# Seven block products instead of eight in the up product of a ConvGeGLU feed-forward stage

## The chip, the cores and the metric

One core of one Trainium2 chip. The metric is device time in microseconds (us) of one execution of the whole kernel; the kernel before takes 887.17 us (median of 3 runs, 887.15 to 887.45).

## The reference

One layer of a hybrid encoder on 512 tokens of width 1024, in float32: a Mamba-2 mixer and an RG-LRU mixer side by side, merged by gates and projected (`w_out`), with a residual; then a feed-forward block. The change lies in the feed-forward block, the last part:

```python
h = rmsnorm(x, ffn_pre_norm[l])                       # [512 tokens, 1024]
up = causal_dwconv(h @ w_ffn_up[l], ffn_conv_w[l], ffn_conv_b[l])   # 6144 channels, 3 taps
f_gate, f_val = jnp.split(up, 2, axis=-1)             # 3072 each
f = (gelu(f_gate, approximate=True) * f_val) @ w_ffn_down[l]
x = x + rmsnorm(f, ffn_post_norm[l])
```

## The kernel before

All large products run in `float32r`. To keep float32 accuracy each operand is split in two, `hi` (a rounded copy, written by ScalarE) and `lo` (what is left, source minus `hi`, by VectorE), and a product is three matmuls: hi x hi, hi x lo, lo x hi (`mm3`, L85). Every matmul has a weight load of its own.

The weights are one stream of slabs of 128x1024 numbers, 512 KB each (`slabs`). `load_slab` (L146) issues the transfer on the SP queue, up to three slabs ahead; `split_slab` (L153) has ScalarE write `whi`, and the low part is queued in `late` and subtracted by VectorE in `low_parts` (L178, L180). `slab` (L182) hands out the next slab and splits ahead. VectorE, ScalarE and TensorE keep the order in which the program is written (`InOrder`, L40; the helper's line is L50), so an instruction that waits holds everything behind it on its engine. GpSimd builds a few constants at the start.

The up stage computes 48 column tiles of 128 channels in pairs: tile i of the gate half and tile i of the value half, 24 pairs (L852). The activations h2 are kept channel-major and split, `h2T` (L797), [128 channels, 8 contraction tiles, 512 tokens]. `up_product` (L828) is one slab against all 512 tokens: 8 contraction tiles x 3 terms = 24 matmuls of 512 columns into one PSUM bank. The first four up products are cut in two halves of 256 tokens: the first halves run as soon as the first two token tiles are normed (L819 to L825, EARLY = 4), the second halves in `up_product`. Behind each product `conv` (L218) has ScalarE scale and shift the PSUM tile into a `tmp` tile and VectorE add the other two taps, reading PSUM. ScalarE then does the gelu of the gate (L855), VectorE multiplies it with the value (L856), and `split` (L195, L197) writes the result as two tiles, which the down product reads as its stationary operand (`facts`, L840).

The down stage is `norm_add` (L700) with 12 slabs per half of the output columns. `use_sqrt` (L864) has ScalarE ready for square roots before it. The slabs are [2 contraction tiles, 512 columns]; each is multiplied for four token tiles. The last three slabs of the second half are taken token tile by token tile, with the norm and the store behind each.

Of the kernel before, what the change touches and what calls it, by code (L numbers as in the profile page):

```python
# [8 lines left out]
F32 = mybir.dt.float32  # L9
F32R = mybir.dt.float32r  # L10
# [24 lines left out]
# columns of the row parameter array  # L35
# [4 lines left out]
class InOrder:  # L40
    """An engine whose instructions keep the order in which they are written here."""
# [12 lines left out]
def block_kernel(ctx: ExitStack, tc, x, slabs, wgate, pc, rows, out):  # L54
    nc = tc.nc
    V, A, PE = (InOrder(tc, e) for e in (nc.vector, nc.scalar, nc.tensor))
    G = nc.gpsimd

# [54 lines left out]
    def step(cost, fn, *args):  # L113
        """A step for the vector engine, of that many microseconds."""
        steps.append((cost, fn, args))

    def next_slab():
        """What follows needs the tensor engine to have gone on, or another engine's result."""
        steps.append(None)
# [21 lines left out]
    n_slabs = slabs.shape[0]  # L141
    stream = {"load": 0, "split": 0, "use": 0}
    raws, splits, places, late = {}, {}, {}, []
    AHEAD, EARLY, WARM = 2, 4, 24

    def load_slab():  # L146
        i = stream["load"]
        if i < n_slabs:
            raws[i] = wts.tile([P, D], F32, tag="raw", name="raw")
            nc.sync.dma_start(out=raws[i], in_=slabs[i])  # L150
            stream["load"] += 1

    def split_slab():  # L153
        i = stream["split"]
        if i >= n_slabs:
            return
        while stream["load"] <= i:
            load_slab()
        raw = raws.pop(i)
        if i == DT_SLAB:  # L160
            hi, lo = wts.tile([P, D], F32R, tag="whi", name="whi"), None
            A.copy(hi, raw)
            h3, r3 = (a.rearrange("p (k c) -> p k c", k=KT)[:, :, 16:32] for a in (hi, raw))
            V.tensor_sub(h3, r3, h3.bitcast(F32))
        else:
            if i in places:
                hi, lo = places[i]()
            else:
                hi = wts.tile([P, D], F32R, tag="whi", name="whi")
                lo = wts.tile([P, D], F32R, tag="wlo", name="wlo")  # L170
            A.copy(hi, raw)
            late.append((lo, raw, hi.bitcast(F32)))
        splits[i] = hi, lo
        stream["split"] += 1
        while stream["load"] < min(n_slabs, stream["split"] + 3):
            load_slab()
# [14 lines left out]
    def prefetch(n):  # L191
        while stream["split"] < min(n_slabs, stream["use"] + n):
            split_slab()
# [54 lines left out]
    def inv_rms(parts, width, e):  # L248
        """(sum of parts / width + e) ** -0.5, as two factors; one part may be [128, n]."""
# [48 lines left out]
    def causal(value, name):  # L298
        m = const.tile([P, P], F32, name=name)      # value where column >= row
# [193 lines left out]
    def carry(c, g):  # L493
        """What earlier chunks bring to this one, and the state after it."""
# [205 lines left out]
    def norm_add(acts, n_slab, e, row, res, tail, lead, target, done):  # L700
        """target = res + RMSNorm(acts @ W) * row; token tile by token tile over the last slabs."""
# [136 lines left out]
    f16 = {}  # L838

    def facts(k):  # L840
        if k < 8:
            kind, key, w = "H", 0, 8
        elif k < 16:
            kind, key, w = "L", 1 + (k - 8) // 4, 4
        else:
            kind, key, w = "Y", 3, 8
        if key not in f16:
            f16[key] = tuple(big16(kind, F32R) if w == 8 else lru8(F32R) for _ in range(2))
        hi, lo = f16[key]
        return hi[:, k % w, :], lo[:, k % w, :]  # L850

    for i in range(NF):  # L852
        gt = conv(up_product(), C_FCW + 3 * i, C_FCB + i, 3)
        vt = conv(up_product(), C_FCW + 3 * (NF + i), C_FCB + NF + i, 3)
        A.activation(gt, gt, AF.Gelu_apprx_tanh)  # L855
        V.tensor_mul(gt, gt, vt)  # L856
        split(*facts(i), gt)

    row_post2 = row_tile(R_POST2)
# [5 lines left out]
    norm_add(facts, 12, EPS1, row_post2, x1s, 3, 0, lambda c, h: tmp(), store)  # L865
# [5 lines left out]
def _layout(x, mix_pre_norm, mix_post_norm, w_in, ssm_conv_w, ssm_conv_b, ssm_dt_bias, ssm_a_log,  # L871
# [5 lines left out]
    def cols(w):  # L877
        """[1024, 128 n]: slab j holds [row in tile, row tile, column] of its 128 columns."""
# [3 lines left out]
    def rws(w):  # L882
        """[K, 1024]: per column half, slabs of two 128-row tiles by 512 columns."""
# [10 lines left out]
    dts = np.zeros((1, P, KT, 8, HEADS), np.float32)     # the dt columns twice, then zeros  # L894
# [17 lines left out]
    def chan(v, n):  # L912
        """[taps, 128 n] to [128, n, taps]."""
# [28 lines left out]
```

## Time and profile before

| | |
|---|---|
| median of 3 runs | 887.17 us |
| span of the profiled execution | 885.8 us |
| median less that span | 1.37 us |
| TensorE busy | 872.5 us, 98% |
| VectorE busy | 519.9 us, 59% |
| ScalarE busy | 392.8 us, 44% |
| GpSimd busy | 1.7 us |
| granted TensorE clock, mean | 0.999 |

The profile is of one execution. It lists its span, from its first to its last instruction; the time of a run also covers what lies around that. PE is TensorE's matmuls, PEld its weight loads, DVE VectorE, ACT ScalarE, POOL GpSimd, SPq the queue of SP, from which the transfers are issued. In a timeline the ends of matmuls are modelled and neighbours overlap, so spacing is read from starts. "L50" is the helper that keeps program order, and stands for the line of most VectorE, ScalarE and TensorE instructions.

### The profile page before, as it was taken

What the parts mean: (1) busy time and instruction counts of PE and PEld (TensorE: products, weight loads), DVE (VectorE), ACT (ScalarE), POOL (GpSimd) and SP (SyncE); (2) the same over time, 40 slices, a digit from 0 to 9 for tenths busy, and PEclk for the clock granted to TensorE, in tenths of its full rate; (3) what the DMA queues carried; (4) which work ended last, traced back from release to release, by engine and by line L of the source; (5) the groups of instructions that cost most, each with busy time, mean ns of one, the idle gap of its engine ahead of it and who ended that gap; (6) DMA issues with size and microseconds to landing.
All of it is one profiled execution on the core that took longest, in us unless ns stands there. A gap on an engine that the chain in (4) does not pass through costs nothing.

```text
span 885.8 us, 10176 instructions
## 1 busy us (share of the span) xinstructions
PE 872.5 (98%) x4050; PEld 724.0 (82%) x4050; DVE 519.9 (59%) x732; ACT 392.8 (44%) x602; POOL 1.7 (0%) x14
## 2 busy tenths in 40 slices
PE   7999999999999999999999999999999999999996
PEld 6888887888878888888888988888888888888885
DVE  6777657987874554344467566666666666223225
ACT  6454535579584334222355444444444444213222
POOL 0000000000000000000000000000000000000000
PEclk9999999999999999999999999999999999999999
DMA  6332232222325332222370022222222222322212
GB/s 224 102 137 95 95 118 84 92 87 72 142 96 182 128 119 72 96 95 95 102 252 27 25 94 96 95 95 96 95 95 95 95 95 95 117 98 95 95 48 96
DMA packets 26192, 91.61 MB, mean 103 GB/s; under 512 B 3040, under 2 KB 4256, under 8 KB 25632
## 3 DMA queue, kind: packets, MB, share of 16 engines
q1 hardware_dynamic: 26144, 90.95, 30.1%
q8 instruction: 32, 0.52, 0.2%
q14 instruction: 16, 0.13, 0.0%
HBM read 88.81 MB, written 2.13 MB: 103 GB/s over the span
## 4 chain that ended last, share of the span: by engine, by line
PE 88%; DVE 5%; ACT 5%; issue 1%; DMA 1%; SPq 0%; DVEq 0%; ACTq 0%
PE ps L50 88%; ACT L L50 1%; DVE L L642 1%; DMA raw<-slabs 1%; DVE wlo L180 1%; ACT whi L50 1%; ACT tmp L50 1%; DVE tmp L660 0%; DVE L L636 0%; ACT L50 0%; ACT junk L245 0%; ACT M L50 0%; DVE Y L197 0%; ACT Y L50 0%; ACT junk L50 0%
## 5 line engine op out<-in xcount | busy, mean ns | idle before, releaser
L180 DVE TENSOR_TENSOR wlo<-raw,whi 128x1024 fp32r<-128x1024 f32 x139 | 169.7, 1222 | 140.5 <-ACT whi L50 137.9
L50 PE MATMUL ps<-C,whi 128*128 128x512 f32 x768 | 241.6, 389 | 0.0
L50 PE MATMUL ps<-H,whi 128*128 128x512 f32 x720 | 224.1, 394 | 1.5 <-DVE H L50 1.5
L50 ACT CAST whi<-raw 128x1024 fp32r<-128x1024 f32 x137 | 143.0, 1045 | 110.9 <-PE ps L50 105.6
L50 PEld LDWEIGHTS ps<-C,whi 128*128 128x128 f32 x768 | 144.1, 188 | 29.9
L225 DVE SCALAR_TENSOR_TENSOR tmp<-ps,pcs,tmp 128x511 f32<-128x511 f32 (+1 forms) x156 | 116.6, 748 | 80.4 <-ACT tmp L50 77.9
L50 PE MATMUL ps<-C,wlo 128*128 128x512 f32 x416 | 161.8, 389 | 0.0
L50 PEld LDWEIGHTS ps<-H,whi 128*128 128x128 f32 x720 | 134.1, 188 | 31.1 <-issue 2.4
L50 PE MATMUL ps<-H,wlo 128*128 128x512 f32 x352 | 137.5, 391 | 0.4 <-DVE wlo L180 0.3
L50 ACT ACTIVATE tmp<-ps,pcs 128x512 f32<-128x512 f32 x68 | 53.1, 780 | 128.2 <-PE ps L50 128.2
L50 PEld LDWEIGHTS ps<-C,wlo 128*128 128x128 f32 x416 | 78.1, 188 | 16.1
L50 PE MATMUL ps<-whi,H 128*128 128x512 f32 x256 | 81.4, 394 | 0.0
L50 PEld LDWEIGHTS ps<-H,wlo 128*128 128x128 f32 x352 | 66.1, 188 | 15.2 <-DVE wlo L180 1.2
L50 PE MATMUL ps<-whi,Y 128*128 128x512 f32 x192 | 59.6, 389 | 0.0
L50 PEld LDWEIGHTS ps<-whi,H 128*128 128x128 f32 x256 | 48.1, 188 | 10.3 <-issue 0.5
L50 PE MATMUL ps<-wlo,H 128*128 128x512 f32 x128 | 49.9, 389 | 0.0
L50 ACT CAST Y<-tmp 128x512 fp32r<-128x512 f32 x24 | 14.9, 621 | 66.9 <-DVE tmp L690 36.8
L50 ACT ACTIVATE tmp<-ps,halfb 128x512 f32<-128x512 f32 x32 | 21.5, 687 | 49.6 <-PE ps L50 49.6
L50 PEld LDWEIGHTS ps<-whi,Y 128*128 128x128 f32 x192 | 36.0, 188 | 7.5
L50 PE MATMUL ps<-Y,whi 128*128 128x512 f32 x128 | 40.5, 396 | 0.2 <-DVE Y L197 0.2
L50 PE MATMUL ps<-whi,L 128*128 128x512 f32 x128 | 39.7, 389 | 0.0
L50 PE MATMUL ps<-wlo,Y 128*128 128x512 f32 x96 | 37.3, 389 | 0.0
(167 smaller groups left out, 848.1 us busy)
## 6 DMA issues: line engine op xcount, KB each, us to landing
raw<-slabs SPq DMA_DIRECT2D x149, 512.0 KB, 3.2
quad<-x SPq DMA_DIRECT2D x8, 512.0 KB, 4.3
M<-acsD SPq DMA_DIRECT2D x4, 1024.0 KB, 4.6
out<-tmp SPq DMA_DIRECT2D x8, 256.0 KB, 2.1
wg<-wgate SPq DMA_DIRECT2D x8, 128.0 KB, 3.3
quad<-rows SPq DMA_DIRECT2D x2, 512.0 KB, 4.7
pcs<-pc SPq DMA_DIRECT2D x1, 178.0 KB, 7.1
acsD<-acsT SPq DMA_DIRECT2D x1, 32.0 KB, 2.9
```

The lines of the kernel that those rows point to most:

```text
L50: return lambda *args, **kw: self.tc.keep_in_program_order(op(*args, **kw))
L180: V.tensor_sub(*late.pop(0))
L225: V.scalar_tensor_tensor(out=t[:, d:], in0=acc[:, :S - d], scalar=pcs[:, w:w + 1], in1=t[:, d:], op0=ALU.mult, op1=ALU.add)
L642: V.tensor_tensor_scan(out=qq[:, e, :], data0=aa[:, e, :], data1=uu[:, e, :], initial=0.0, op0=ALU.mult, op1=ALU.add)
```

## The change

Two slabs of a pair are read as a matrix of 2 x 2 blocks: slab pair (gate, value) by depth half (contraction tiles 0 to 3 and 4 to 7), a11, a12, a21, a22. The activations are cut in depth half by token half. For pairs 3 to 23 the up product of a pair is formed from seven products of blocks ([128 channels x 512 deep] by [512 deep x 256 tokens]) in Winograd's form of Strassen's scheme. Pairs 0 to 2 stay as they were (`PLAIN = 3`).

For the weights it forms s1 = a21 + a22, s2 = s1 - a11, s4 = a11 - a21, s3 = a12 - s2 per pair, on GpSimd, which gets a program-ordered handle `GP`. Seven blocks are split (s1, s2, s3, s4, a11, a12, a22): `hi` on ScalarE, `lo` on VectorE for five and on GpSimd for a12 and a22. For the activations it once rebuilds h2 from its two parts (`h_whole`, eight adds of 128x512 on GpSimd), forms four combinations (`h_sums`, four of 128x1024) and splits them (`h_split`).

The products of a pair are added up by VectorE and ScalarE into two SBUF tiles, `oa` (gate) and `ob` (value), which `conv` now reads in place of PSUM. `seven` spreads a pair over seven slots, one block product each; the splits for the next pair, and the conv, gelu and multiplication of the pair before, are written between them. A pair's last block product (a22) runs in slot 4 of the next pair. The weights of a pair come by one transfer of 1 MB into one half of a two-pair ring.

The results of the up stage are kept unsplit (`f_tile`), and `f_split` splits them during the down stage: `norm_add` calls `turn(kp)` ahead of each slab of its first half, `down_turn`, which also finishes pair 23. The layout of the slabs and the work before the feed-forward block are unchanged. In the diff removed comments are left out.

```diff
@@ norm_add
-    def norm_add(acts, n_slab, e, row, res, tail, lead, target, done):
+    def norm_add(acts, n_slab, e, row, res, tail, lead, target, done, turn=None):
...
             for kp in range(n_slab - n_end):
+                if turn and j == 0:
+                    turn(kp)
                 w = slab(AHEAD if j else AHEAD + lead * kp)
@@ up stage
...
-    for i in range(NF):
-        gt = conv(up_product(), C_FCW + 3 * i, C_FCB + i, 3)
-        vt = conv(up_product(), C_FCW + 3 * (NF + i), C_FCB + NF + i, 3)
-        A.activation(gt, gt, AF.Gelu_apprx_tanh)
-        V.tensor_mul(gt, gt, vt)
-        split(*facts(i), gt)
-    row_post2 = row_tile(R_POST2)
...
+    ring, fH = big16("H", F32), big16("H", F32)
+    fY = [big16("Y", F32), big16("Y", F32)]
+    def f_tile(i):
+        return fH[:, i, :] if i < 8 else fY[i // 8 - 1][:, i % 8, :]
...
+    HT, HK = S // 2, KT // 2
+    T0, T1 = slice(0, HT), slice(HT, S)
+    whole = fY[1]
+    sums4 = fY[0].rearrange("p (m h) s -> p m (h s)", m=4)
+    tsum = [sums4[:, m, :].rearrange("p (k t) -> p k t", k=HK) for m in range(4)]
+    comb = {}
+    def h_whole(k):
+        GP.tensor_add(whole[:, k, :], h2T[0][:, k, :].bitcast(F32), h2T[1][:, k, :].bitcast(F32))
+    def h_sums(m):
+        b11, b12, b21, b22 = (whole[:, a:a + HK, t] for a in (0, HK) for t in (T0, T1))
+        t1, t2, t3, t4 = tsum
+        GP.tensor_sub(*((t1, b12, b11), (t2, b22, t1), (t3, b22, b12), (t4, b21, t2))[m])
+    def h_split(m):
+        t = lru8(F32R).rearrange("p k (two t) -> p k two t", two=2)
+        comb[m] = t[:, :, 0, :], t[:, :, 1, :]
+        split(comb[m][0], comb[m][1], tsum[m])
+    def plain_block(half, t):
+        return tuple(h[:, half * HK:(half + 1) * HK, t] for h in h2T)
+    def block_product(out, w, b, start=False):
+        for k in range(HK):
+            c = slice(k * P, (k + 1) * P)
+            for e, (u, v) in enumerate(((0, 0), (0, 1), (1, 0))):
+                PE.matmul(out, lhsT=w[u][:, c], rhs=b[v][:, k, :], start=start and k == e == 0,
+                          stop=k == HK - 1 and e == 2, skip_group_check=not start)
...
+    def pair_load(n):
+        if n >= NF:
+            return
+        raw = pairs[:, n % 2, :]
+        nc.sync.dma_start(out=raw.rearrange("p (i c) -> p i c", i=2),
+                          in_=slabs[UP_SLAB + 2 * n:UP_SLAB + 2 * n + 2].rearrange("i p c -> p i c"))
+        blk[n] = {q: raw[:, e * S:(e + 1) * S] for e, q in enumerate(("a11", "a12", "a21", "a22"))}
...
+    def w_sum(n, q):
+        if n >= NF:
+            return
+        b = blk[n]
+        b[q] = unit("raw", n % 2 if q == "s1" else {"s2": 2, "s4": 3, "s3": 4}[q])
+        if q == "s1":
+            GP.tensor_add(b[q], b["a21"], b["a22"])
+        else:
+            GP.tensor_sub(b[q], *((b["s1"], b["a11"]), (b["a11"], b["a21"]), (b["a12"], b["s2"]))[int(q[1]) - 2])
+    ORDER = ("a11", "s2", "s4", "s3", "a12", "s1")
...
+    def w_split(n, q):
+        if n >= NF:
+            return
+        b = blk[n]
...
+        A.copy(hi, b[q])
+        (GP if q in ("a22", "a12") else V).tensor_sub(lo, b[q], hi.bitcast(F32))
+        b["w" + q] = hi, lo
+    row_post2 = quad()
+    mid = row_post2.rearrange("p (e t) -> p e t", e=4)
+    pr = {}
+    def gate_part(n):
+        p = pr[n]
+        p["g"] = conv(p["oa"], C_FCW + 3 * n, C_FCB + n, 3)
+    def gelu_part(n):
+        f_gate(pr[n]["g"])
+    def last_product(n):
+        block_product(pr[n]["z"][:, T1], blk[n]["wa22"], comb[3])
+    def value_part(n):
+        p = pr.pop(n)
+        V.tensor_add(p["ob"][:, T0], p["u2"], p["z"][:, T1])
+        vt = conv(p["ob"], C_FCW + 3 * (NF + n), C_FCB + NF + n, 3)
+        f_done(n, p["g"], vt)
+    def seven(n):
+        b, p = blk[n], pr.setdefault(n, {})
+        old = n - 1 if n - 1 in pr else None
+        x, z = ps(), ps()
+        p["z"] = z
+        if n % 2 == PLAIN % 2:
+            p["w"] = ps()
+        else:
+            p["w"] = pr[n - 1]["w"]
+        w = p["w"][:, (T0, T1)[(n - PLAIN) % 2]]
+        block_product(x[:, T0], b["wa11"], plain_block(0, T0), True)
+        pair_load(n + 2)
+        w_sum(n + 1, "s1")
+        w_split(n, "s1")
+        if old is not None:
+            gate_part(old)
+        yield
+        block_product(x[:, T1], b["ws2"], comb[1])
+        w_split(n + 1, "a11")
+        w_sum(n + 1, "s2")
+        p["u2"] = mid[:, n % 2, :]
+        A.copy(p["u2"], x[:, T0])
+        yield
+        block_product(z[:, T0], b["ws4"], plain_block(1, T1), True)
+        V.tensor_add(p["u2"], p["u2"], x[:, T1])
+        w_split(n + 1, "s2")
+        w_sum(n + 1, "s4")
+        if old is not None:
+            gelu_part(old)
+        yield
+        block_product(z[:, T1], b["ws3"], comb[2])
+        w_split(n + 1, "s4")
+        w_sum(n + 1, "s3")
+        yield
+        if old is not None:
+            last_product(old)
+        w_split(n + 1, "s3")
+        w_split(n + 1, "a22")
+        yield
+        block_product(x[:, T0], b["wa12"], plain_block(1, T0))
+        if old is not None:
+            value_part(old)
+        yield
+        new = (n - PLAIN) % 2 == 0
+        block_product(w, b["ws1"], comb[0], new)
+        w_split(n + 1, "a12")
+        p["oa"], p["ob"] = tmp(), tmp()
+        A.copy(p["oa"][:, T0], x[:, T0])
+        u4 = mid[:, 2 + n % 2, :]
+        V.tensor_add(u4, p["u2"], w)
+        V.tensor_add(p["oa"][:, T1], z[:, T0], u4)
+        V.tensor_add(p["ob"][:, T1], z[:, T1], u4)
...
+    def f_split(i):
+        split(*f_parts(i), f_tile(i))
+    for i in range(PLAIN):
+        acc = up_product()
+        if i == 0:
+            for k in range(KT):
+                h_whole(k)
+            pair_load(PLAIN)
+            pair_load(PLAIN + 1)
+        elif i == 1:
+            for m in range(4):
+                h_sums(m)
+        if i == PLAIN - 1:
+            for q in ("s1", "s2"):
+                w_sum(PLAIN, q)
+            h_split(1)
+            w_split(PLAIN, "a11")
+        gt = conv(acc, C_FCW + 3 * i, C_FCB + i, 3)
+        acc = up_product()
+        if i == PLAIN - 1:
+            for q in ("s4", "s3"):
+                w_sum(PLAIN, q)
+            w_split(PLAIN, "s2")
+            w_split(PLAIN, "s4")
+            h_split(2)
+            w_split(PLAIN, "s3")
+            w_split(PLAIN, "a22")
+            w_split(PLAIN, "a12")
+            h_split(0)
+            h_split(3)
+        vt = conv(acc, C_FCW + 3 * (NF + i), C_FCB + NF + i, 3)
+        f_gate(gt)
+        f_done(i, gt, vt)
+    for n in range(PLAIN, NF):
+        for slot, _ in enumerate(seven(n)):
+            if n < NF - 1:
+                continue
+            if slot == 0:
+                for k in stream:
+                    stream[k] = DOWN_SLAB
+                end[0] = slabs.shape[0]
+                first = big16("H", F32R).rearrange("p (i w h) s -> p i w (h s)", i=2, w=2)
+                places.update({DOWN_SLAB + e: (lambda e=e: (first[:, e, 0, :], first[:, e, 1, :]))
+                               for e in range(2)})
+                load_slab()
+                load_slab()
+            elif slot == 3:
+                f_split(0)
+                f_split(1)
+            elif slot == 4:
+                split_slab()
+                low_parts()
+            elif slot == 5:
+                f_split(2)
+                f_split(3)
+    def down_turn(kp):
+        n = NF - 1
+        if kp == 0:
+            gate_part(n)
+            gelu_part(n)
+        elif kp == 1:
+            last_product(n)
+            value_part(n)
+            nc.sync.dma_start(out=row_post2,
+                              in_=rows[0:1, R_POST2:R_POST2 + D].partition_broadcast(P))
+        for i in (2 * kp + 4, 2 * kp + 5):
+            if i < NF:
+                f_split(i)
     def store(c, h, o):
         nc.sync.dma_start(out=out[c * P:(c + 1) * P, h * S:(h + 1) * S], in_=o)
     use_sqrt()
-    norm_add(facts, 12, EPS1, row_post2, x1s, 3, 0, lambda c, h: tmp(), store)
+    norm_add(f_parts, 12, EPS1, row_post2, x1s, 3, 0, lambda c, h: tmp(), store, down_turn)
```

## Rows read from the trace of the kernel before

**Rows 1.** Page, busy us (share of the span) and instructions of each engine
```profile
PE 872.5 (98%) x4050; PEld 724.0 (82%) x4050; DVE 519.9 (59%) x732; ACT 392.8 (44%) x602; POOL 1.7 (0%) x14
```

**Rows 2.** Chain that ended last, in time: start us, us, what; from 480 us
```profile
479.95 399.05 PE ps L50 x1860
...
881.30 0.75 DVE tmp L741
```

**Rows 3.** Windows, two pairs of the up stage: busy us (instructions), clock, DMA
```profile
600.00:610.87 10.87, 10.87 (x49) 9.01 (x48) 6.74 (x9) 4.58 (x7) 0.00 (x0) 1.00 0.31 96
610.87:621.74 10.87, 10.87 (x49) 9.00 (x48) 6.74 (x9) 4.59 (x7) 0.00 (x0) 1.00 0.27 99
```

**Rows 4.** Timeline of VectorE in two pairs: start, us, what, [idle before]
```profile
607.84 1.54 DVE L225 SCALAR_TENSOR_TENSOR tmp<-ps,pcs,tmp 128x511 f32<-128x511 f32 x2 [2.77 <-ACT tmp L50]
609.48 0.69 DVE L856 TENSOR_TENSOR tmp<-tmp 128x512 f32<-128x512 f32 x1
...
618.72 1.53 DVE L225 SCALAR_TENSOR_TENSOR tmp<-ps,pcs,tmp 128x511 f32<-128x511 f32 x2 [2.77 <-ACT tmp L50]
```

**Rows 5.** Timeline of TensorE in the early up products, 256 columns each
```profile
484.11 8.79 PE L50 MATMUL ps<-C,L 128*128 128x256 f32 x72
...
494.72 14.32 PE L50 MATMUL ps<-C,L 128*128 128x256 f32 x118
```

**Rows 6.** Groups by line and form, 450 to 680 us: busy, mean ns | idle before
```profile
L50 ACT ACTIVATE tmp<-ps,pcs 128x512 f32<-128x512 f32 x35 | 27.3, 781 | 73.1 <-PE ps L50 73.1
L225 DVE SCALAR_TENSOR_TENSOR tmp<-ps,pcs,tmp 128x511 f32<-128x511 f32 x35 | 26.2, 750 | 50.5 <-ACT tmp L50 50.5
...
L50 PE MATMUL ps<-C,L 128*128 128x256 f32 x192 | 23.4, 283 | 0.0
...
L856 DVE TENSOR_TENSOR tmp<-tmp 128x512 f32<-128x512 f32 x17 | 11.8, 692 | 2.1 <-ACT tmp L50 0.4
L50 ACT ACTIVATE tmp<-tmp 128x512 f32<-128x512 f32 x17 | 10.6, 621 | 0.0
...
L202 DVE SCALAR_TENSOR_TENSOR C<-ps,pcs,C 128x256 fp32r<-128x256 f32 x16 | 7.0, 477 | 2.4 <-ACT C L201 2.4
L201 ACT ACTIVATE C<-ps,pcs 128x256 fp32r<-128x256 f32 x16 | 6.7, 475 | 5.2 <-PE ps L50 4.0 <-DVE C L202 1.3
...
L197 DVE TENSOR_TENSOR L<-tmp,L 128x512 fp32r<-128x512 f32 x8 | 5.5, 692 | 5.5 <-ACT L L50 5.5
...
L50 ACT CAST L<-tmp 128x512 fp32r<-128x512 f32 x8 | 5.0, 621 | 15.0 <-DVE tmp L856 15.0
...
L732 DVE TENSOR_TENSOR tmp<-ps,quad 128x512 f32<-128x512 f32 x4 | 2.7, 685 | 2.2 <-ACT junk L245 2.2
```

**Rows 7.** Timeline at the change from the up to the down stage
```profile
752.28 1.28 ACT L50 ACT_TABLE_LOAD   x1
...
754.75 2.36 DVE L180 TENSOR_TENSOR wlo<-raw,whi 128x1024 fp32r<-128x1024 f32 x2 [1.76 <-ACT whi L50]
```

**Rows 8.** Groups of GpSimd by form: busy us, mean ns | idle before
```profile
L301 POOL TENSOR_SCALAR_AFFINE_SELECT quart<-quart 128x128 f32<-128x128 f32 x1 | 0.3, 293 | 0.0
...
L232 POOL MEMSET eps<- 128x1 f32 x3 | 0.2, 99 | 0.0
```

**Rows 9.** Page, DMA issues: count, KB each, median us from issue to landing
```profile
raw<-slabs SPq DMA_DIRECT2D x149, 512.0 KB, 3.2
...
M<-acsD SPq DMA_DIRECT2D x4, 1024.0 KB, 4.6
```

**Rows 10.** Timeline at the start of the up stage: last part of h2T, first full-width matmuls
```profile
497.35 0.48 DVE L202 SCALAR_TENSOR_TENSOR C<-ps,pcs,C 128x256 fp32r<-128x256 f32 x1 [0.54 <-ACT C L201]
...
508.88 0.63 PE L50 MATMUL ps<-C,whi 128*128 128x512 f32 x2
```

**Rows 11.** Waits of VectorE, 530 to 750 us: us in total, times, longest
```profile
DVE tmp L225 <- ACT tmp L50: 62.9, 40, 2.8
```

More of the change, by code (lines that the diff above doesn't have):

```diff
@@ L25 @@
 DT_SLAB = 1
+UP_SLAB = 77
+DOWN_SLAB = UP_SLAB + 2 * NF
+PLAIN = 3
 C_SCW, C_SCB = 0, 48
@@ L57, in block_kernel @@
     G = nc.gpsimd
+    GP = InOrder(tc, nc.gpsimd)
     const = ctx.enter_context(tc.tile_pool(name="const", bufs=1))
@@ L138, in tick @@
             fn(*args)
-    n_slabs = slabs.shape[0]
     stream = {"load": 0, "split": 0, "use": 0}
     raws, splits, places, late = {}, {}, {}, []
+    end = [UP_SLAB + 2 * PLAIN]
     AHEAD, EARLY, WARM = 2, 4, 24
@@ L147, in load_slab @@
         i = stream["load"]
-        if i < n_slabs:
+        if i < end[0]:
             raws[i] = wts.tile([P, D], F32, tag="raw", name="raw")
@@ L154, in split_slab @@
         i = stream["split"]
-        if i >= n_slabs:
+        if i >= end[0]:
             return
@@ L174, in split_slab @@
         stream["split"] += 1
-        while stream["load"] < min(n_slabs, stream["split"] + 3):
+        while stream["load"] < min(end[0], stream["split"] + 3):
             load_slab()
@@ L191, in prefetch @@
     def prefetch(n):
-        while stream["split"] < min(n_slabs, stream["use"] + n):
+        while stream["split"] < min(end[0], stream["use"] + n):
             split_slab()
@@ L837, in block_kernel @@
     A.on = True
[L838 to L844, printed above, removed]
-        else:
[L846 to L850, printed above, removed]
-    for i in range(NF):
-        gt = conv(up_product(), C_FCW + 3 * i, C_FCB + i, 3)
-        vt = conv(up_product(), C_FCW + 3 * (NF + i), C_FCB + NF + i, 3)
-        A.activation(gt, gt, AF.Gelu_apprx_tanh)
-        V.tensor_mul(gt, gt, vt)
-        split(*facts(i), gt)
@@ L859, in block_kernel, with f_gate, f_done @@
-    row_post2 = row_tile(R_POST2)
+    ring, fH = big16("H", F32), big16("H", F32)
+    fY = [big16("Y", F32), big16("Y", F32)]
+    def f_tile(i):
+        return fH[:, i, :] if i < 8 else fY[i // 8 - 1][:, i % 8, :]
+    def f_gate(gt):
+        A.activation(gt, gt, AF.Gelu_apprx_tanh)
+    def f_done(i, gt, vt):
+        V.tensor_mul(f_tile(i), gt, vt)
+    HT, HK = S // 2, KT // 2
+    T0, T1 = slice(0, HT), slice(HT, S)
+    whole = fY[1]
+    sums4 = fY[0].rearrange("p (m h) s -> p m (h s)", m=4)
@@ new lines, in plain_block @@
+    def plain_block(half, t):
[6 more added lines that the diff above has]
+                          stop=k == HK - 1 and e == 2, skip_group_check=not start)
+    pairs = ring.rearrange("p (n i) s -> p n (i s)", n=2)
@@ new lines, in block_kernel, with unit @@
+    blk = {}
+    def pair_load(n):
[5 more added lines that the diff above has]
+        blk[n] = {q: raw[:, e * S:(e + 1) * S] for e, q in enumerate(("a11", "a12", "a21", "a22"))}
+    room = {}
+    def unit(kind, i):
+        key = kind, i // 2
+        if key not in room:
+            room[key] = wts.tile([P, D], F32 if kind == "raw" else F32R, tag=kind, name=kind)
+        return room[key][:, i % 2 * S:(i % 2 + 1) * S]
@@ new lines, in w_sum @@
+    def w_sum(n, q):
[5 more added lines that the diff above has]
+            GP.tensor_add(b[q], b["a21"], b["a22"])
+        else:
+            GP.tensor_sub(b[q], *((b["s1"], b["a11"]), (b["a11"], b["a21"]), (b["a12"], b["s2"]))[int(q[1]) - 2])
+    ORDER = ("a11", "s2", "s4", "s3", "a12", "s1")
+    spare = []
+    def w_split(n, q):
+        if n >= NF:
+            return
+        b = blk[n]
+        if q == "a22":
+            if not spare:
+                spare.append(work.tile([P, 2, 2, S], F32R, tag="M", name="a22", bufs=1))
+            hi, lo = (spare[0][:, n % 2, e, :] for e in range(2))
+        else:
+            hi, lo = (unit(kind, ORDER.index(q)) for kind in ("whi", "wlo"))
+        A.copy(hi, b[q])
+        (GP if q in ("a22", "a12") else V).tensor_sub(lo, b[q], hi.bitcast(F32))
+        b["w" + q] = hi, lo
@@ new lines, in block_kernel, with f_parts @@
+    parts = {}
+    def f_parts(i):
+        key = i // 4 if i < 8 or i >= 16 else 2
+        if key not in parts:
+            if key < 2:
+                parts[key] = lru8(F32R), lru8(F32R)
+            elif key == 2:
+                parts[key] = big16("C", F32R), big16("C", F32R)
+            else:
+                t = big16("H", F32R)
+                parts[key] = t[:, 0:4, :], t[:, 4:8, :]
+        return tuple(t[:, i % 8 if key == 2 else i % 4, :] for t in parts[key])
+    def f_split(i):
+        split(*f_parts(i), f_tile(i))
@@ new lines, in block_kernel @@
+    assert stream["use"] == UP_SLAB + 2 * PLAIN
+    for n in range(PLAIN, NF):
[20 more added lines that the diff above has]
+                f_split(3)
```

## The prediction

> **What bounds the kernel now.** I read the busy shares first, then the chain that ended last, then the up stage by stretches, by groups of instructions and by timeline. TensorE is busy 98% of a span of 885.8 us, VectorE 59%, ScalarE 44%, and GpSimd does nothing after its first microseconds [rows 1]. The chain is one unbroken piece of matmuls from 479.95 us on, 399.05 us long, and only the norm of the last token tile follows it [rows 2]. So in the up stage the time is the number of matmuls times their spacing, and nothing that another engine saves there counts. Two stretches of 10.87 us, one pair of slabs each, show TensorE full, VectorE at 6.74 us and ScalarE at 4.58 us, at granted clock 1.00, its upper level, 2.4 GHz [rows 3]. The first taps of two neighbouring pairs start at 607.84 and 618.72: the period is 10.88 us for 48 matmuls of 512 columns, 226.7 ns each [rows 4].
>
> **TensorE.** The change gives a pair 7 block products x 4 contraction tiles x 3 terms = 84 matmuls of 256 columns. The trace has such matmuls, in the early up products, each with its own weight load: 118 in 14.32 us, the last one 0.283 us long, so (14.32 - 0.283) / 117 = 120.0 ns each; 72 in 8.79 us give 119.8 [rows 5, 6]. Half the columns cost 53% of the time, not 50%. A pair takes 84 x 0.120 = 10.08 us instead of 10.88, which is 0.80 less, or 7.4% instead of the 12.5% that seven for eight suggests. Over 21 pairs: **-16.8 us**, if TensorE stays full.
>
> **Does VectorE fit in 10.08 us?** Per pair it gets: five low parts (s1, a11, s2, s4, s3) of 128x512 at 0.692 = 3.46; four conv taps, as two dependent couples of 1.54 = 3.08; the gate product 0.69; five adds of 256 columns. The slab and activation splits go (two of 1.22 and one of 0.69; the latter move to the down stage). A 256-column add is not in the trace; half of the 0.685 add from PSUM is 0.34, the 256-column multiply-add from PSUM is 0.477 [rows 6]. I take 0.45, near the row of its width: 2.25. Sum 9.48. Neighbours that don't depend on each other overlap by some 0.08 (two of 1.22 take 2.36 [rows 7]), about six times, -0.5; and in the value half it waits for ScalarE between the add and the taps, 0.62 + 0.1 [rows 6]. So **9.7 us** of 10.08. It comes in two parts. From the end of last_product (slot 4) it does add 0.45, wait 0.7, taps 1.54, product 0.8, = 3.5 us, then the three adds of the seventh product 1.3: it ends 1.9 us into the next pair. Ahead of the next last_product, at 7.2, stand s1, two taps, a11, u2, s2, s4, s3: 0.69 + 1.54 + 3.46 less overlaps = 5.2, ending at 7.1. It holds, with 0.1 to 0.4 us to spare and with the 0.34 us adds 0.9. TensorE sees none of VectorE's delay while that holds, because each weight buffer is split one slot after its last use and read six slots (8.6 us) later.
>
> **ScalarE**: seven 512-column copies at 0.621 = 4.35, two of 256 at 0.475, two conv scalings at most 0.781, the gelu 0.62: 7.5 us of 10.08 [rows 6]. Hidden.
>
> **GpSimd** gets six two-input operations of 128x512 per pair. The trace has none. Its nearest rows are one-input: 0.293 us for 128x128, 0.099 for a 128x1 [rows 8]. Scaling only the part above the fixed 0.099 gives 0.875; four times the row gives 1.17; both inputs read one after the other, 2.34. I take 1.17, the row scaled whole: 7.0 us per pair, hidden; it becomes the bound above 10.08 / 6 = 1.68. The Trainium skill's GPSIMD Engine Reference, section 3.1, states 4497 ns for a two-input add of 2048 columns; a quarter of it, 1.12 us, is an estimate from that page, and by it the sum would not move.
>
> **Transfers**: one of 1 MB per pair instead of two of 0.5. It may start when the last reader of its half of the ring, the a12 low part on GpSimd, is done, some 0.5 us into a pair; the trace's 1 MB transfers land after 4.6 us [rows 9]; it is read at 10.08. 4 to 5 us to spare. SP has nothing else queued in these pairs.
>
> **Start.** h2T is complete at 497.83 and the full-width matmuls begin at 508.88 [rows 10]; so the pair before the first block product ends at 508.88 + 10.88 = 519.8. GpSimd must do eight adds (9.4 us), four of 1024 columns (9.4), then s1, s2, s4, s3 (4.7): 521.4. Needed: s2 at 521.2, s4 at 522.6, s3 at 524.1, and each is split within 1.4 us behind its sum: just in time. VectorE, though, has behind s3 two activation splits (2.4), the conv of the third pair (1.5), its product (0.7) and only then s1: 523.4 + 5.3 = 528.9; the seventh product wants it at 519.8 + 5 x 1.44 = 527.0 (this pair has no last_product ahead of it). **+2 us**, bounds 0 and 8 (GpSimd at 1.5 us instead of 1.17 shifts the chain by 6).
>
> **Hand-over to down.** The split of fact 4 stands on VectorE ahead of the low parts of the second and third down slab, and goes into the buffer of the activation block that last_product(23) reads, which runs only after the first down slab's matmuls. So TensorE waits after it for two splits of 0.69 and a slab's 1.22 = **+2.6 us**, bounds 0 and 4. The 48 fact splits moved into the first ten down slabs add there 1.4 us of VectorE and 1.2 of ScalarE to 5.4 us each: hidden. Gelu and Sqrt alternate once more, 1.28 us of table each [rows 7], on ScalarE while it has slack; the tail is untouched.
>
> **Sum**: -16.8 + 2 + 2.6 = -12.2 on a span of 885.8: 873.6. The median of the runs stands 1.4 above the profiled execution's span (887.17), so **875 us**, own range 870 to 883.
>
> **Rivals.**
> *A, GpSimd and VectorE get in each other's way: slower.* For: GpSimd has been idle throughout, so no row shows a VectorE operation beside it, and 0.1 to 0.4 us of slack is all there is; ten of the fifteen VectorE operations of a pair read two SBUF operands (3.46 + 3.08 + 0.69 = 7.2 us) and GpSimd is to be active 7.0 us. If the two take turns whole, a pair takes 7.2 + 7.0 = 14.2 us, less if the 256-column adds are what runs beside: 21 x (14.2 - 10.88) + 5 = +75, 962 us. If VectorE runs at half speed where they overlap (7.0 x 0.72 = 5.0 us), it takes 9.7 + 2.5 = 12.2: +33, 920 us, which is the case I price it at. It decides early: a stretch of the 7.2 us by 0.9 us, some 12%, eats the whole gain. Against: nothing measured here.
> The Trainium skill's SBUF — State Buffer, section Who interferes with whom, speaks for this: a VectorE instruction with two SBUF inputs and a GpSimd one that reads SBUF exclude each other for a whole instruction; by that rule the sum would be the 962 us above. No run here shows it yet.
> *B, GpSimd is the bound.* At the upper bound of 2.34 us, 14.0 us per pair: 21 x 3.2 + 8 = +74, 961 us. For: two inputs. Against: the one-input rows at 0.2 to 0.3 us.
> *C, VectorE's in-order chain is just too long:* with another semaphore delay of 0.05 us at each of fifteen operations it takes 10.5, and 21 x (10.5 - 10.88) + 5 = -3; at 10.65 nothing is left, 887 us. For: 62.9 us of waits for ScalarE in the stage now, in stretches of up to 2.8 [rows 11], which this schedule has no room for. Against: they are waits for the product, which come from TensorE's pace.
> That the change does less than it says I leave out: the count of matmuls follows from the loops.
>
> **How the numbers follow.** Forecast 0.50; A 0.34; B 0.04; C 0.12. Under 0.2%, 1.8 us, a measurement can't tell a change from none. Faster: the forecast's 0.50 and 0.05 of C, 0.55. Same: 0.05 of C, 0.02 of A, 0.07. Slower: 0.32 of A, 0.04 of B, 0.02 of C, 0.38. The range goes from 868 (with neither stall it is 887.2 - 16.8 = 870.4; 2 us below that for a gain at the hand-over that I don't see) to 925, past the half-speed case of A; the whole of taking turns and B lie outside, about 0.2. The likeliest case's own range is 870 to 883.
>
> **What would show it.** Matmuls of 256 columns at 120 ns without gaps between block products, and last taps of neighbouring pairs 10.1 us apart, confirm the first step. VectorE's 128x512 low parts must still take 0.69 us: at 0.9 or more, with TensorE waiting for a low part, A is true and I am wrong. GpSimd's 128x512 rows, start to start, over 1.68 us would be B. Waits of TensorE of 2 us near 527 and 2.6 us at the first down slabs show the two stalls. VectorE rows at today's lengths, with TensorE waiting once per pair for a low part, would be C.

## The result, and the profile after

Slower: 958.38 us (median of 4 runs, 958.22 to 959.26) against 887.31 for the kernel before on the same chip, a ratio of 1.079 (95% interval 1.078 to 1.081). I had forecast 875 with a range up to 925. The time lies near rival A in its whole-turns form, 962, which the range left out; that it lies so near is partly luck, as the part on the prediction shows.

The page's busy shares after (busy us, share of the span of 957.6, instructions), to be set against [rows 1]:

```profile
PE 884.0 (92%) x4806; PEld 767.3 (80%) x4806; DVE 651.7 (68%) x904; ACT 450.7 (47%) x755; POOL 212.9 (22%) x152
```

TensorE is no longer full. Four rows of the waits of TensorE over the whole run (releaser; us in total, times, longest):

```profile
PE ps L53 <- DVE quad L984: 46.9, 19, 8.3
PE ps L53 <- DVE tmp L1011: 6.5, 6, 1.1
PE ps L53 <- ACT H L53: 3.4, 1, 3.4
...
PE ps L53 <- DVE wlo L937: 0.8, 1, 0.8
```

TensorE waits once a pair, some 2 us, for VectorE's add at L984. The wait for a low part (L937), which I had named as the sign of rival A, hardly occurs. VectorE's groups by form in the middle of the up stage, 560 to 800 us, answer to [rows 6]: there the low part took 692 ns, each tap about 750 and the product 692.

```profile
L937 DVE TENSOR_TENSOR wlo<-raw,whi 128x512 fp32r<-128x512 f32 x71 | 59.1, 854 | 6.1 <-ACT whi L53 6.1
L229 DVE SCALAR_TENSOR_TENSOR tmp<-tmp,pcs 128x511 f32<-128x511 f32 x35 | 43.1, 1232 | 24.3 <-ACT tmp L53 24.3
L229 DVE SCALAR_TENSOR_TENSOR tmp<-tmp,pcs 128x510 f32<-128x510 f32 x35 | 41.6, 1187 | 0.6
L856 DVE TENSOR_TENSOR Y<-tmp 128x512 f32<-128x512 f32 x13 | 21.2, 1632 | 0.4
...
L956 DVE TENSOR_TENSOR tmp<-quad,ps 128x256 f32<-128x256 f32 x18 | 7.5, 414 | 0.0
```

Operations with two SBUF operands got longer; the add that reads PSUM (L956) did not grow with them: without GpSimd, in experiment 1, it takes 418 ns. How, is to be seen in the timelines of GpSimd and then of VectorE (start, duration, line, operation):

```profile
638.95 1.62 POOL L53 TENSOR_TENSOR raw<-raw,H 128x512 f32<-128x512 f32 x1
640.65 1.63 POOL L53 TENSOR_TENSOR raw<-H,raw 128x512 f32<-128x512 f32 x1
642.24 1.30 POOL L53 TENSOR_TENSOR raw<-H 128x512 f32<-128x512 f32 x1
```

```profile
639.67 1.45 DVE L937 TENSOR_TENSOR wlo<-raw,whi 128x512 fp32r<-128x512 f32 x1
641.05 0.41 DVE L1010 TENSOR_TENSOR tmp<-ps,quad 128x256 f32<-128x256 f32 x1
641.38 0.41 DVE L1011 TENSOR_TENSOR tmp<-ps,quad 128x256 f32<-128x256 f32 x1
642.41 1.68 DVE L229 SCALAR_TENSOR_TENSOR tmp<-tmp,pcs 128x511 f32<-128x511 f32 x1 [0.62 <-ACT tmp L53]
644.01 0.68 DVE L937 TENSOR_TENSOR wlo<-H,whi 128x512 fp32r<-128x512 f32 x1
644.61 0.74 DVE L229 SCALAR_TENSOR_TENSOR tmp<-tmp,pcs 128x510 f32<-128x510 f32 x1
645.27 0.41 DVE L984 TENSOR_TENSOR quad<-quad,ps 128x256 f32<-128x256 f32 x1
```

GpSimd's first operation ends at 638.95 + 1.62 = 640.57; VectorE's low part, begun at 639.67, ends at 641.12, 0.55 later. GpSimd's third ends at 643.54; the tap, begun at 642.41, ends at 644.09, again 0.55 later. The two adds from PSUM lie beside GpSimd's second operation at their 0.41. With GpSimd done, low part and tap are back at 0.68 and 0.74. So a two-operand VectorE operation that meets a GpSimd one ends nearly as if it had begun when that one ended.

The whole trace from 540 to 800 us agrees. VectorE has 187 operations there that read two SBUF operands. 79 of them begin while a GpSimd operation runs, and all 79 end 0.54 to 0.62 us after it. The other 108 take 0.68 to 0.75 us. GpSimd waits in the same way: its 97 operations that begin while such a VectorE operation runs take 1.34 to 1.75 us, the other 17 take 1.29 to 1.30. Whichever of the two begins first goes first.

TensorE in this pair, by windows (busy us and count of PE, PEld, DVE, ACT, POOL; granted clock, DMA share, GB/s):

```profile
640.00:645.70 5.70, 3.70 (x31) 3.50 (x30) 5.08 (x8) 2.38 (x5) 3.46 (x3) 1.00 0.26 108
645.70:650.00 4.30, 4.27 (x23) 4.27 (x24) 3.04 (x6) 3.52 (x7) 1.66 (x2) 0.60 0.00 0
650.00:655.00 5.00, 5.00 (x43) 5.00 (x43) 4.97 (x5) 0.62 (x1) 4.84 (x4) 1.00 0.56 178
```

It waits 2.03 us until 645.73, and then works 4.3 us at a granted clock of 0.60, a stretch partly at 1.2 GHz: 4.3 x 0.4 = 1.7 us more. Matmuls 217 ns apart there are 120 ns apart from 650.2 on. The same add releases TensorE at 645.73 and at 659.58, a period of 13.85 us = 10.1 of matmuls + 2.0 of wait + 1.7 of clock. This divides TensorE's time, not the causes: in experiment 6 the clock stays at 1.00, and a pair still takes 13.1 us.

Over the run the first L984 add stands at 536.3 and the 21st at 807.2: 20 periods of 13.55 us, against 10.88 [rows 4]: +53.4. The start costs 11.2: the block product that waits begins at 536.8, and by the prediction's count it would begin at 525.6 without stalls. Of that, 1.7 were lost before the changed code, in the first full-width matmul at 510.56 instead of 508.88 [rows 10]; executions differ there, and experiments 2 and 5 show 508.6 and 508.7.

```profile
510.56 0.63 PE L53 MATMUL ps<-C,whi 128*128 128x512 f32 x2
...
536.81 0.80 PE L53 MATMUL ps<-C,whi 128*128 128x256 f32 x2 [8.32 <-DVE quad L984]
```

The spans differ by 71.8, which leaves 7.2 for the hand-over and the rest.

### The profile page after: what moved, and what is told of

It reads as the page before. It is cut to its first block, busy times and chain, and to the rows that moved or that the text cites. A ratio compares the mean times of both kernels' runs of the same rounds, so it can differ in the third digit from the quotient of the medians.

```text
span 957.6 us, 12293 instructions
## 1 busy us (share of the span) xinstructions
PE 884.0 (92%) x4806; PEld 767.3 (80%) x4806; DVE 651.7 (68%) x904; ACT 450.7 (47%) x755; POOL 212.9 (22%) x152
## 4 chain that ended last, share of the span: by engine, by line
PE 55%; DVE 23%; ACT 9%; issue 8%; POOL 2%; DMA 1%; SPq 0%; ACTq 0%; DVEq 0%; POOLq 0%
PE ps L53 55%; DVE tmp L229 8%; DVE wlo L937 4%; ACT tmp L53 4%; DVE Y L856 2%; ACT whi L53 2%; POOL Y L53 2%; ACT L L53 1%; DVE L L646 1%; DMA raw<-slabs 1%; DVE H L856 1%; DVE wlo L184 1%; DVE tmp L1010 1%; DVE tmp L956 1%; DVE L L201 1%
## 5 line engine op out<-in xcount | busy, mean ns | idle before, releaser
L53 ACT CAST whi<-raw 128x1024 fp32r<-128x1024 f32 (+1 forms) x177 | 147.4, 843 | 118.1 <-PE ps L53 106.7
L53 PE MATMUL ps<-C,whi 128*128 128x256 f32 (+1 forms) x600 | 138.6, 318 | 47.0 <-DVE quad L984 46.9
L53 PE MATMUL ps<-L,whi 128*128 128x256 f32 (+1 forms) x568 | 126.4, 309 | 0.0
L53 POOL TENSOR_TENSOR Y<-C 128x512 f32<-128x512 f32 x8 | 10.1, 1304 | 493.8 <-DVE C L206 493.8
L229 DVE SCALAR_TENSOR_TENSOR tmp<-tmp,pcs 128x511 f32<-128x511 f32 x84 | 98.9, 1178 | 28.1 <-ACT tmp L53 27.3
L53 PE MATMUL ps<-C,wlo 128*128 128x256 f32 (+1 forms) x332 | 107.0, 322 | 0.0
L53 PEld LDWEIGHTS ps<-L,whi 128*128 128x128 f32 x568 | 98.4, 208 | 2.5
L937 DVE TENSOR_TENSOR wlo<-raw,whi 128x512 fp32r<-128x512 f32 x84 | 72.1, 879 | 7.6 <-ACT whi L53 7.6
L53 PE MATMUL ps<-L,wlo 128*128 128x256 f32 x252 | 74.9, 297 | 0.8 <-DVE wlo L937 0.8
L53 POOL TENSOR_TENSOR raw<-H 128x512 f32<-128x512 f32 x42 | 66.4, 1581 | 0.0
L229 DVE SCALAR_TENSOR_TENSOR tmp<-ps,pcs,tmp 128x511 f32<-128x511 f32 (+2 forms) x72 | 53.7, 745 | 14.9 <-ACT tmp L53 14.0
```

The costliest lines, as they stand in the source:

```text
L53: return lambda *args, **kw: self.tc.keep_in_program_order(op(*args, **kw))
L229: V.scalar_tensor_tensor(out=t[:, d:], in0=acc[:, :S - d], scalar=pcs[:, w:w + 1], in1=t[:, d:], op0=ALU.mult, op1=ALU.add)
L937: (GP if q in ("a22", "a12") else V).tensor_sub(lo, b[q], hi.bitcast(F32))
```

## The experiments

In the expectations T says that a VectorE operation with two SBUF operands and a GpSimd one that reads SBUF take turns, each for a whole operation; R1 that VectorE's order of work is too long by itself; R1b that the wait comes from the shared PSUM bank; R2 that any GpSimd work slows VectorE.

**1. No GpSimd work in the pairs.**

```diff
+    filled = set()
...
-        if q == "s1":
+        if (q, n % 2 if q == "s1" else 0) not in filled:
+            filled.add((q, n % 2 if q == "s1" else 0))
             GP.tensor_add(b[q], b["a21"], b["a22"])
-        else:
-            GP.tensor_sub(b[q], *((b["s1"], b["a11"]), (b["a11"], b["a21"]), (b["a12"], b["s2"]))[int(q[1]) - 2])
...
-        (GP if q in ("a22", "a12") else V).tensor_sub(lo, b[q], hi.bitcast(F32))
+        if q in ("a22", "a12"):
+            b["w" + q] = hi, hi
+            return
+        V.tensor_sub(lo, b[q], hi.bitcast(F32))
```

> Leaves out the six GpSimd operations of each pair (the four weight sums are written once and then stay, the low parts of a12 and a22 are left out), so the numbers that it computes are not the reference's; matmuls, ScalarE and VectorE work stay. Theory T (a VectorE operation with two SBUF operands and a GpSimd operation that reads SBUF take turns, whole instruction by whole instruction): VectorE's 128x512 low parts are back at 0.69 us and the taps at 0.75, the period of a pair falls from 13.9 to 10.1 to 10.4 us, the time is 868 to 885 us. Rival R1 (VectorE's chain of a pair is too long by itself, with its wait for ScalarE and TensorE's wait for the same PSUM bank): the period stays above 10.9, the time above 890 us.

884.57 us, 0.996 of before (0.995 to 0.997). The same 40 us of the up stage in the changed kernel and then in this one, and VectorE's low parts in this one:

```profile
600.00:640.00 40.00, 34.07 (x243) 33.47 (x242) 34.93 (x45) 19.57 (x36) 25.81 (x18) 0.87 0.19 65
```

```profile
600.00:640.00 40.00, 40.00 (x336) 40.00 (x335) 33.48 (x60) 26.51 (x48) 0.00 (x0) 1.00 0.31 104
```

```profile
L940 DVE TENSOR_TENSOR wlo<-raw,whi 128x512 fp32r<-128x512 f32 x68 | 45.3, 687 | 5.7 <-ACT whi L53 5.7
```

336 matmuls in 40 us are 10.0 us a pair, and TensorE is full. By form, 560 to 800 us, the low part (the line above) takes 687 ns, first taps 751, the product 690. 74 us of time went with GpSimd's operations, so R1 falls. But the 875 isn't reached; experiments 8 and 9 look for what is missing.

**2. GpSimd busy, but only writing.** As 1, with three memsets where each sum and each of its low parts stood (`for _ in range(3): GP.memset(b[q], 0.01)`).

> Each of the six GpSimd operations of a pair is replaced by three fills of the same 128x512 tile, which write SBUF and read nothing, so the numbers are not the reference's. GpSimd is to be busy some 9 us per pair as in the changed kernel. T in its narrow form (the shared thing is the reading of SBUF): VectorE rows at 0.69 and 0.75, time within 6 us of the run without GpSimd work. Rival R2 (any GpSimd work beside VectorE slows it, by its writes or its instruction stream): rows of 0.85 to 1.6 us and a time over 930.

884.67 us, 0.997 (0.995 to 0.998). The same window, where the column before the clock is GpSimd, and GpSimd's memsets by form, 560 to 800 us:

```profile
600.00:640.00 40.00, 40.00 (x336) 40.00 (x335) 33.12 (x61) 25.72 (x48) 36.42 (x73) 1.00 0.30 103
```

```profile
L53 POOL MEMSET raw<- 128x512 f32 x197 | 100.9, 527 | 7.6
```

GpSimd is busy 36.4 of 40 us and costs nothing: R2 falls. ScalarE's copies still wait for GpSimd's writes here, so a late result of GpSimd's is not the cause either. What the memsets lack, and the six operations have, is reading.

**3. The six operations on VectorE** (`GP` becomes `V` in `w_sum` and `w_split`).

> The same computation, the six GpSimd operations of a pair put on VectorE instead. T: VectorE gets 6 x 0.69 = 4.1 us more of work and loses 3.6 us of waiting for turns, all rows at 0.69 to 0.75; it bounds at 13.3 to 14.2 us per pair, time 945 to 968: taking turns with GpSimd costs VectorE as much as doing the work itself. If GpSimd cost VectorE nothing (R1), the pair would grow by 4.1 us to 18 and the time to over 1030.

907.64 us, 1.022 (1.020 to 1.024): a miss, I had VectorE's sum too high. Its 40 us window:

```profile
600.00:640.00 40.00, 36.44 (x300) 35.83 (x299) 40.00 (x74) 21.61 (x41) 0.00 (x0) 1.00 0.31 106
```

VectorE is the bound, 40.00 of 40, and a pair takes 11.5 us (L1009 at 601.52 and 613.04). So the same six operations cost the pair 2 us less on the engine that had no time for them than on the idle one.

**4. The kernel before with GpSimd reads added.** Six subtractions into a scratch tile behind each pair from pair 3, whose result nobody reads.

```diff
+    scr = work.tile([P, S], F32, tag="junk", name="scr", bufs=1)
...
+        if i >= 3:
+            for k in range(6):
+                G.tensor_sub(scr, vt, h2T[0][:, k, :].bitcast(F32))
```

> The kernel before, with six GpSimd subtractions of 128x512 from SBUF to a scratch tile added to each pair from the fourth on; nothing reads their result. T: TensorE stays the bound, since VectorE has 4.1 us of slack per pair: 886 to 892 us; but VectorE's operations with two SBUF operands (low parts, the gate product) stretch where GpSimd runs and end 0.5 to 0.6 us (512 columns) or 1.1 us (1024) behind the GpSimd instruction, while the taps, which read PSUM and one SBUF tile, stay at 0.75. If the stretch belongs to the seven-product schedule alone, all rows stay as before.

888.59 us, 1.000 (0.999 to 1.001). The slab's low part in the kernel before, 450 to 680 us, and then this run's groups by form over the same stretch, beside [rows 6]:

```profile
L180 DVE TENSOR_TENSOR wlo<-raw,whi 128x1024 fp32r<-128x1024 f32 x33 | 40.3, 1221 | 4.3 <-ACT whi L50 4.1 <-ACT whi L171 0.2
```

```profile
L861 POOL TENSOR_TENSOR scr<-tmp,C 128x512 f32<-128x512 f32 x81 | 139.5, 1722 | 538.9 <-DVE tmp L225 533.5 <-POOL scr L861 0.2
L180 DVE TENSOR_TENSOR wlo<-raw,whi 128x1024 fp32r<-128x1024 f32 x33 | 68.7, 2082 | 0.5 <-ACT whi L50 0.5
L225 DVE SCALAR_TENSOR_TENSOR tmp<-ps,pcs,tmp 128x511 f32<-128x511 f32 x35 | 26.1, 745 | 24.1 <-ACT tmp L50 24.1
...
L857 DVE TENSOR_TENSOR tmp<-tmp 128x512 f32<-128x512 f32 x17 | 11.8, 692 | 2.1 <-ACT tmp L50 0.4
```

The slab's low part went from 1.22 to 2.08 us with nothing else changed; the tap, which in this kernel reads PSUM, stayed at 0.745. The gate product (L857), which reads two SBUF operands, was expected to grow too and did not: in nearly every pair GpSimd's first operation begins while the product runs, and then it is GpSimd that waits. VectorE's busy time in 600 to 640 rose from 24.76 to 33.85 us of 40 and TensorE stayed full: here, where VectorE has time to spare, the clash costs none.

**5. Another PSUM bank.** L984 reads one half of a bank into whose other half the waiting block product writes.

```diff
-        x, z = ps(), ps()
+        x, y, z = ps(), ps(), ps()
...
-        block_product(x[:, T1], b["ws2"], comb[1])
+        block_product(y[:, T1], b["ws2"], comb[1], True)
...
-        V.tensor_add(p["u2"], p["u2"], x[:, T1])
+        V.tensor_add(p["u2"], p["u2"], y[:, T1])
```

> The changed kernel, with the second block product of a pair in a PSUM bank of its own, so that the sixth (into x) no longer waits until VectorE has read the second. T: VectorE bounds, blocked by GpSimd; TensorE waits elsewhere for as long, the pair stays at 13.3 to 13.9 us, 943 to 960 us. Rival R1b (the wait for that bank, 47 us in all, and the lower clock after it are the loss): the pair falls to 10.1 to 10.5 and the time to 880 to 895 us.

958.57 us, 1.079 (1.078 to 1.081). The first of TensorE's waits:

```profile
PE ps L53 <- DVE tmp L1011: 46.2, 20, 5.0
```

The wait has moved to another add, with nearly the same total. The bank only decides where TensorE meets VectorE's delay; R1b falls.

**6. Four operations on GpSimd instead of six** (the two low parts on VectorE).

> The changed kernel, with the low parts of a12 and a22 on VectorE; GpSimd keeps the four weight sums. T, with six GpSimd operations at 13.86 us per pair and none at 11.5: in between, 13.1 us by a straight line, 936 to 950 us. If GpSimd took work off VectorE as intended, 1.2 us more work on VectorE would make it slower than the 958 us of the changed kernel.

948.92 us, 1.068 (1.067 to 1.069), inside what T gave:

```profile
600.00:640.00 40.00, 32.04 (x256) 30.69 (x254) 39.28 (x52) 19.56 (x37) 18.82 (x12) 1.00 0.25 83
```

256 matmuls in 40 us make 84 / 256 x 40 = 13.1 us a pair. TensorE's first two waits over the run:

```profile
PE ps L53 <- DVE quad L984: 30.4, 19, 7.6
PE ps L53 <- DVE tmp L1011: 24.0, 18, 1.4
```

TensorE waits about twice a pair, 54.4 us in all against 53.4 in the changed kernel, but most of them are shorter, and the granted clock in the window is 1.00. Taking 2 x 0.69 us of work back onto the full VectorE shortened the pair.

**7. Expensive and cheap pairs in turn.** No GpSimd in the pairs, and some of them by seven products (S), the others by eight (P) with 512-column matmuls out of the same ring, so that VectorE's mean load fits. Alternating, ten S:

```diff
+    KINDS = "xxxPSPSPSPSPSPSPSPSPSPSP"
...
-            GP.tensor_add(b[q], b["a21"], b["a22"])
+            V.tensor_add(b[q], b["a21"], b["a22"])
...
+        halves = wide(g, n, ("a11", "a12"))
```

> A version meant to win: every second pair from 4 to 22 by seven products (10 pairs), the others by plain 512-column products out of the same ring; all weight sums and low parts on VectorE, none on GpSimd. VectorE needs 11.5 us for the one (as measured with all on VectorE) and about 5.8 for the other, 17.3 of the 20.96 us that TensorE needs: TensorE bounds again. 10 x 0.80 = 8.0 us less, 0 to 4 us for start and hand-over: 879 to 884 us. If VectorE's waits don't fit, TensorE waits and the clock falls after it: 890 or more.

881.55 us, 0.992 (0.991 to 0.993): faster than both kernels, with the whole computation done. Its window:

```profile
600.00:640.00 40.00, 40.00 (x250) 36.17 (x249) 33.41 (x59) 20.82 (x36) 0.00 (x0) 1.00 0.28 99
```

TensorE is full and VectorE has a sixth of its time free. Four pairs take 41.93 us (VectorE's add at L1054 stands at 620.82 and at 662.75) against 43.52 [rows 4]. With two S to one P, thirteen S (`"xxxPSSPSSPSSPSSPSSPSSPSP"`):

> As the alternating version, with two of three pairs by seven products (13 pairs, 10.4 us less). VectorE needs 2 x 11.5 + 5.8 = 28.8 of 31.0 us. If it fits: 877 to 883 us. If the two neighbouring pairs outrun the slack that the plain one gives back, TensorE waits in each of them, loses clock after it, and it is slower than the alternating version: 885 to 895 us. I hold the second for likelier.

881.59 us, 0.992 (0.991 to 0.994): it fits VectorE, against what I held likelier, but three more S pairs brought nothing measurable. Its trace shows where most of their 2.4 us went: TensorE waits for the add at L1054 twice, at the start and near 695 us, and by the starts of its matmuls loses 1.3 and 0.7 us there.

**8. A later start of the seven products.** Experiment 1 with PLAIN = 5 and the four activation splits spread over pairs 2 and 3.

> The run without GpSimd work per pair (it leaves out the same part of the computation), with the first block product two pairs later and the four activation splits moved out of the last plain pair, so that nothing stands ahead of the first weight splits. In that run TensorE waited 4.8 us at the start and its clock fell to 0.55 to 0.77 for 10 us behind it, 3.4 us more. If these 8.2 us are the start's price: they fall to under 1, and two pairs by eight products cost 1.6 us back: 884.6 - 7.2 + 1.6 = 879, range 877 to 881. If the clock falls there for another reason than the wait, it stays under 1 in this stretch and the time is 881 to 884.

878.17 us, 0.988 (0.986 to 0.990), as expected. In experiment 1 TensorE's timeline at the start has this wait, and two windows the clock around it:

```profile
521.34 0.40 PE L53 MATMUL ps<-C,whi 128*128 128x256 f32 x2
...
532.52 2.93 PE L53 MATMUL ps<-C,whi 128*128 128x256 f32 x12 [4.26 <-DVE quad L987]
...
537.61 0.40 PE L53 MATMUL ps<-C,whi 128*128 128x256 f32 x2
```

```profile
530.00:535.00 5.00, 2.48 (x11) 2.48 (x12) 4.27 (x8) 1.50 (x3) 0.00 (x0) 0.55 0.00 0
535.00:540.00 5.00, 5.00 (x35) 5.00 (x34) 2.14 (x5) 2.73 (x5) 0.00 (x0) 0.77 0.52 168
```

The expectation's 8.2 us counts part of the loss twice, since the clock is low while TensorE still waits. Starts give it once. The first block product begins at 521.34, so the one that waits would begin four block products later, after 48 matmuls of 120 ns, at 527.1; it begins at 532.52, 5.4 us late. The next 24 matmuls take 5.09 us, to 537.61, instead of 2.88: 2.2 for the clock. Together 7.6. With the later start neither is there:

```profile
525.00:545.00 20.00, 20.00 (x98) 16.84 (x96) 13.07 (x17) 9.15 (x15) 7.38 (x4) 1.00 0.02 2
```

**9. The hand-over.** Experiment 1 with the fact splits one slab later (`for i in (2 * kp + 2, 2 * kp + 3): if 4 <= i < NF`).

> The run without GpSimd work per pair, with the splits of facts 4 and on moved behind the last block product of the last pair, by one down slab. There TensorE waited 3.0 us and the clock fell to 0.50 for some 5 us, 3.4 us more. If the order on VectorE is the cause, the wait falls to under 1 us, the clock stays up: 884.6 - 5 = 879 to 881. If something else holds the second down slab (its transfer or ScalarE), no change: 884 to 885.

882.57 us, 0.994 (0.992 to 0.996): half a miss. The wait fell from 3.0 to 2.0 us only. ScalarE's timeline there shows what is left:

```profile
742.93 1.28 ACT L53 ACT_TABLE_LOAD   x1 [1.65 <-DVE tmp L229]
744.22 0.63 ACT L53 ACTIVATE tmp<-tmp 128x512 f32<-128x512 f32 x1
744.76 1.03 ACT L53 CAST H<-raw 128x1024 fp32r<-128x1024 f32 x1
```

The last pair's gelu, with the table loaded for it, stands ahead of the copy of the down slab that TensorE needs at 745.84.

## Why the prediction was wrong, point by point

**TensorE: right.** 120.0 ns a matmul, 10.08 us a pair: experiments 1 and 2 show 10.0, and 40.00 of 40 us busy.

**"Does VectorE fit in 10.08 us?": the step that failed.** The sum of durations, 9.7 with 0.7 of waits, was sound, if a little high: with GpSimd's reads away VectorE is busy 33.5 of 40 us, 8.4 a pair, and TensorE never waits for it in mid-stage. What failed was carrying durations from a trace with an idle GpSimd into a schedule where it is active, mostly reading SBUF, 25.8 of 40 us. Experiments 1, 2 and 4 together show the mechanism of rival A: the same work of VectorE without GpSimd's reads, without harm; GpSimd busy but not reading, without harm; operations that read added to the kernel before, and the low parts grow. By timeline it is whole turns, not half speed: I had priced A at the milder case, 12.2 us a pair, where whole turns gave 14.2 and 13.55 came. That 962 came so near is partly luck: it holds 69.7 for the pairs, where 53.4 came, and 5 for the start and the hand-over, where 18.4 came. Its 14.2 lets every two-operand operation of VectorE take turns with all of GpSimd's work; 79 of 187 met a GpSimd operation. The sign that I had named for A, low parts at 0.9 or more with TensorE waiting for one, failed in both halves, though A is true. The low parts' mean is 0.855, because 69 of the 89 between 560 and 800 us meet no GpSimd operation and take 0.68; the 20 that meet one take 1.45. TensorE is not seen waiting for a low part, since the delay adds up along VectorE's queue and reaches TensorE at whichever add comes next (experiment 5). VectorE's order in the up stage is also not the written one, as I had described it, but the scheduler's (`V.on = False`, L299), which for example puts a low part between the adds of L1009 and L1010.

The Trainium skill's SBUF — State Buffer, section Who interferes with whom, had it: a VectorE instruction with two SBUF inputs excludes a GpSimd one that reads SBUF for a whole instruction. The traces agree on each point: 0.54 to 0.62 us from GpSimd's end to VectorE's, in all 79 cases; operations that read PSUM unharmed (0.41, 0.745); 884.67 us with a writing GpSimd against 884.57 without.

**GpSimd "hidden": wrong in its effect, not its length.** Its eight activation adds start 1.25 us apart (I took 1.17), beside VectorE operations that read PSUM; in mid-stage its groups average 1.35 to 1.62. It never was the bound: it waited 84 us in all for ScalarE's copies. Rival B is out.

**Rival C** is out in mid-stage. **ScalarE and the transfers** were hidden in mid-stage, as said: 1 MB landed after 4.9 us, 4.6 forecast.

**Start, 2 forecast: undersized.** 7.6 without GpSimd in the pairs, 5.4 of it by the end of the wait; with it 9.5 by the end of the wait (11.2 less the 1.7). The order I had named is there, and experiment 8, which changes it, removes the loss. But experiment 8 also starts later, so it doesn't separate the order from the clash with GpSimd's sums of the activations, beside which a 128x512 product of VectorE took 2.89 us in experiment 1. I priced the wait alone, and the seventh product as the first victim where it was the sixth; the clock behind the wait cost 2.2 more.

**Hand-over, 2.6 forecast: undersized.** TensorE's timeline there in experiment 1:

```profile
744.67 1.59 PE L53 MATMUL ps<-L,a 128*128 128x256 f32 x12
748.51 0.50 PE L53 MATMUL ps<-H,L 128*128 128x512 f32 x1 [2.25 <-ACT H L53]
749.77 8.32 PE L53 MATMUL ps<-H,L 128*128 128x512 f32 x23 [0.76 <-DVE H L184]
757.93 0.39 PE L53 MATMUL ps<-whi,L 128*128 128x512 f32 x1
```

By starts, 3.4 us are lost around the two waits, and the 23 matmuls behind them take 8.16 us instead of 23 x 0.2267 = 5.2, at a granted clock of 0.50 from 750 to 755: 3.0 more, 6.4 in all. I had VectorE's splits as what TensorE waits for; the longer wait was for ScalarE. That the table swap falls where ScalarE "has slack" was wrong by experiment 9.

With mid-stage right and these two at their measured size the sum is -16.8 + 7.6 + 6.4 = -2.8. Experiment 1's span is 1.3 us below that of before, but its first full-width matmul comes 1.55 later (510.43 against 508.88), ahead of all this: -2.8 + 1.55 = -1.25. The ratio of its runs says 3.7 below. So even without the clash 875 would have been missed.

## What to carry to other kernels

An idle GpSimd is no free place for two-operand SBUF work while VectorE does the same kind: a VectorE operation that meets a GpSimd one waits until that has ended, 1.45 us instead of 0.68 for a low part here, so work that VectorE does in 0.69 us can be cheaper left there (11.5 us a pair against 13.55). Leave GpSimd operations that only write, or run it beside VectorE work that reads PSUM. When an exchange of TensorE time for VectorE time overdraws VectorE, make it on a part of the tiles, so that VectorE's mean load fits (0.992 here). When a wait of TensorE is priced, look at the granted clock behind it too: in experiment 1 the lower clock cost 2.2 us behind 5.4 of waiting at the start and 3.0 behind 3.4 at the hand-over; behind the shorter waits of experiment 6, from 600 to 640 us, it did not fall.

## What the runs showed of the hardware that was not expected

Behind a wait of 2 us the granted clock was 0.60 over the next 4.3 us; in experiments 3 and 6, where the waits are 1.2 to 1.6 us in the mean, it is 1.00 from 600 to 640 us. A GpSimd subtraction of 128x512 grew too, to 1.72 us in experiment 4 against 1.29 for one that meets no two-operand VectorE operation in the changed kernel, while memsets of that size stayed at 0.527 beside a VectorE busy 33 of 40 us.
